# Every second step's key products as three fp32r passes in the cache stage of a two-layer decoder step

## The chip, the cores and the metric

The kernel runs on one core of a Trainium2 chip. The metric is device microseconds of one execution, first to last work of the program; the numbers of runs are medians. Instructions of five engines run side by side: TensorE (PE, its weight loads PEld), VectorE (DVE), ScalarE (ACT), GpSimd (POOL) and SyncE (SP). Each engine takes its own queue in order.

## The reference, cut to what matters

Two layers; in each, 1024 prompt tokens and 8 samples of 4 tokens. The stage that is changed is the samples' attention over a paged cache of 8192 positions:

```python
def key_nope(ckv, w_uk, kn_g):                      # ckv: [..., 128], w_uk: [128, 4*64]
    k = (ckv @ w_uk).reshape(ckv.shape[:-1] + (N_HEADS, NOPE))
    return rmsnorm(k, kn_g)                         # over the 64 of a head, fp32
...
def step(carry, pt):                                # over pages
    lat = cache_latent[layer, pt]; krp = cache_krope[layer, pt]
    kn = key_nope(lat, w_uk, kn_g)
    s = attn_scores(qn, qr, kn, krp)                # qn.kn + qr.kr, times a scale
    ... running max, exp, sums; acc += p @ lat
```

So each cached latent (128 numbers) is multiplied by `w_uk`, the mean square of its 64 numbers per head is taken, and its score with 4 heads x 4 tokens = 16 queries is scaled by the root of that. The 16 scores come out of the same product: the query is folded into `w_uk` beforehand, which gives 16 more columns.

## The kernel before, in words

A cache stage (`sample_attn`) stands in each layer between the projections and the prompt's attention. It works on 16 units (`u`), half a sample's cache each: 4096 latents, gathered by an indirect DMA on GpSimd's queue into one of 8 large slots, once as `latc` (for turning) and once as `lat` (for the value product), with the rotary keys `kr`. A unit has 8 steps (`q`, `tau = 8u + q`), a step 4 tiles of 128 latents:

- `T`: VectorE turns 512 columns of `latc` into `lT`, three steps ahead.
- `K`: per tile one fp32 product of `lT` with `WK` (256 key columns and 16 query columns, `KPC` = 272), two tiles to a pair of PSUM banks `kproj` (three such pairs). An fp32 product is two PE instructions in the trace, an fp32r product one. ScalarE squares the 256 into `sq`, `nope` copies the 16 scores into `nope`.
- `tree`: GpSimd adds the two halves of each head's squares; `red`: VectorE sums the rest into `ms`.

Around these, work of the unit before (`hp`) and of the one before that (`hpp`) is laid in at fixed steps: `krT`, `lnexp`, `newton`, `rope` (rotary scores, PE), `scale` (GpSimd), `addrope`, `colmax`, `maxT`, `bcast`, `expo`; then `expo_act`, `rowsum`, `pv` (the value product, PE), `pvend`. In layer 0 every second unit up to 13 also does a piece of the modulation weights (`ada_step`: 16 PE instructions at step 4, a copy at 5, four turns at 6). Units 13 to 15 prepare the prompt's first head (`warm`). The order is written out by hand (a manual schedule): every engine's queue is the program's order. Helpers `add`, `sub`, `mul` take the engine as last argument (`v` VectorE, `g` GpSimd) and show as L104; `act` shows as L101.

Some parts of the kernel already use three fp32r passes in place of an fp32 product: `split` copies a high part with ScalarE and subtracts it for the low part; `mm3` does high x high, high x low, low x high (L214 to L216).

Of the kernel before, what the change touches and what calls it, by code (L numbers as in the profile page):

```python
# [23 lines left out]
NT = 4  # L24
# [23 lines left out]
def _build(nc, tc, a, ctx):  # L48
# [105 lines left out]
    WKR = cp.tile([128, 2, 256], F32R, name="WKR")  # L154
    WK = [cp.tile([128, KPC], F32, name=f"WK{i}") for i in range(2)]
# [123 lines left out]
    def load_small_w(l, r, wp, pool):  # L279
# [8 lines left out]
        split(WKR[:, 0], WKR[:, 1], w[:, 768:1024])  # L288
        for i in range(2):
            v.tensor_copy(WK[i][:, 0:256], w[:, 768:1024])  # L290
# [41 lines left out]
    def mla_tile(l, r, raw, rc, m, pool, qk, cT_, nxt, vout=None):  # L332
# [18 lines left out]
        mm3(pk[:, 0:256], cT_[:, 0, sl], cT_[:, 1, sl], WKR[:, 0], WKR[:, 1])  # L351
# [129 lines left out]
    def sample_attn(l, keep, pool, warm):  # L481
# [4 lines left out]
        pbuf = [keep.tile([128, 528], F32, tag=f"p{i}", name=f"p{i}") for i in range(2)]  # L486
# [21 lines left out]
        def gather_kr(u):  # L508
            if u < NU:
                if not krs:  # L510
                    krs.append(slot("krs"))
                H[u].kr = krs[0][:, u % 4, 0:1024]
                rows(u, H[u].kr, "kr")

        def new_wk(b):
            if b < NB:
                v.tensor_copy(WK[b % 2][:, 256:KPC], S.qa[:, b].rearrange("p h t -> p (h t)"))

        def T(tau):
            if tau >= NU * NSTEP:  # L520
                return
            h, q = H[tau // NSTEP], tau % NSTEP
            h.lT = getattr(h, "lT", {})
            h.lT[q] = pool.tile([128, 512], F32, tag="lT", name="lT", bufs=4)
            v.transpose(h.lT[q], h.latc[:, 512 * q:512 * q + 512])  # L525
            if q == NSTEP - 1:
                h.latc = None

        def K(h, q, j):
            if q == 0 and j == 0:  # L530
                h.nope = keep.tile([128, 32, NH, NT], F32, tag="nope", name="nope", bufs=3)
                h.ms = keep.tile([128, 32, NH], F32, tag="ms", name="ms", bufs=2)
            if j == 0:
                h.sq = pool.tile([128, 4, 256], F32, tag="sq", name="sq", bufs=3)
            wk = WK[h.b % 2]
            kp = ps2("kproj")
            lT = h.lT[q]
            for i in range(2):
                t = 2 * j + i
                sl = slice(t * 128, (t + 1) * 128)  # L540
# [8 lines left out]
        def tree(h, q):  # L549
            sv = h.sq.rearrange("p n (h x d) -> p (n h) x d", h=NH, x=2)  # L550
            t32 = pool.tile([128, 16, 32], F32, tag="t32", name="t32", bufs=3)
            add(t32, sv[:, :, 0, :], sv[:, :, 1, :], g)
            halves.append((h, q, t32))

        def red():
            h, q, t32 = halves.pop(0)
            v.tensor_reduce(h.ms[:, 4 * q:4 * q + 4, :].rearrange("p n (h o) -> p (n h) o", o=1), t32, AX.X, ALU.add)  # L557

        def krT(h, c):
            t = pool.tile([128, 512], F32, tag="krT", name="krT", bufs=2)  # L560
            v.transpose(t, h.kr[:, 512 * c:512 * c + 512])
            h.krT = getattr(h, "krT", []) + [t]

        def rope(h, c):
            if c == 0:
                h.pr = (psr if h is H.get(NU - 1) else psm)("ropesc")
            for k in range(4):
                o = 64 * (4 * c + k)
                te.matmul(h.pr[:, o:o + 64], h.krT[c][:, 128 * k:128 * k + 128], BD[:, h.b, :], start=True, stop=True)  # L569

        def lnexp(h):
            h.t0 = keep.tile([128, 32, NH], F32, tag="ta", name="ta", bufs=2)
            act(h.t0, h.ms, AF.Ln, scale=1.0 / NOPE, bias=epsT)
            act(h.t0, h.t0, AF.Exp, scale=-0.5)

        def newton(h):
            h.rs = keep.tile([128, 32, NH], F32, tag="rs", name="rs", bufs=2)
            mul(h.rs, h.t0, h.t0)
# [24 lines left out]
        def expo(h, u):  # L603
            scv = h.sc.rearrange("p (n r) -> p n r", r=16)
            sub(scv, scv, h.pm[:, 128:144].unsqueeze(1).to_broadcast([128, 32, 16]))

        def expo_act(h, u):
            act(pbuf[u % 2][:, 0:512], h.sc, AF.Exp)

        def rowsum(h, u):  # L610
            v.tensor_reduce(RS[:, u % 2, :, u // 2, :].unsqueeze(3),
                            pbuf[u % 2][:, 0:512].rearrange("p (n h t) -> p h t n", h=NH, t=NT), AX.X, ALU.add)

        def pv(h, u, q):
            p = pbuf[u % 2]
            if q == 0:
                h.po = (psm if u == NU - 2 else psr)("po")
            for j in range(4):
                t = 4 * q + j
                te.matmul(h.po[32 * j:32 * j + 32, 0:128], p[:, 16 * t:16 * t + 32], h.lat[:, t * 128:(t + 1) * 128],  # L620
                          start=(q == 0), stop=(q == 7))

        def pvend(h, u):
            v.tensor_copy(O[:, u, :], h.po[:, 0:128])
# [5 lines left out]
        def ada_step(u, q):  # L630
# [10 lines left out]
            elif q == 5:  # L641
                A.mg = pool.tile([128, 512], F32, tag="adamg", name="adamg")
# [7 lines left out]
        gather_kr(1)  # L650
        new_wk(0)
        T(0)
        T(1)
        T(2)
        new_wk(1)
        for i in range(2):
            v.memset(pbuf[i][:, 512:528], 0.0)
        for tau in range(NSTEP * NU):
            u, q = divmod(tau, NSTEP)
            h, pu = H[u], u - 1  # L660
# [4 lines left out]
            if tau > 1:  # L665
                red()
            if hp is not None:
                if q < 2:
                    krT(hp, q)
# [8 lines left out]
            nope(h, q, 1, kp)  # L678
            if hp is not None:
                if q == 1:  # L680
                    lnexp(hp)
                elif q in (2, 3):
                    rope(hp, q - 2)
                    if q == 2:
                        scale(hp)
                elif q == 6:
                    maxT(hp, pu)
                elif q == 7:
                    bcast(hp, pu)
                    expo(hp, pu)  # L690
            if hpp is not None:
                if q == 0:
                    expo_act(hpp, u - 2)
                elif q == 3:
                    rowsum(hpp, u - 2)
                    for i in range(8):
                        pv(hpp, u - 2, i)
                elif q == 4:
# [7 lines left out]
            if u == NU - 1 and q in (4, 6):  # L706
                krT(h, q // 2 - 2)
# [5 lines left out]
        def tail():  # L713
# [3 lines left out]
            red()  # L717
# [977 lines left out]
```

## Time and profile before

| | us |
|---|---|
| median of 3 runs (range) | 1606.57 (1605.94 to 1606.84) |
| the profiled execution's own time | 1606.35 |
| its span in the trace | 1604.6 |
| cache stage of layer 0, of layer 1, first to last key product | 320.8 to 634.9, 1111.0 to 1408.1 |
| PE busy | 1547.2 (96%) |
| VectorE, ScalarE, GpSimd busy | 1122.6, 790.4, 743.8 |

The profile's spans of matmuls overlap one another, because the engine is pipelined: what one costs is read from start to start. A span of VectorE or GpSimd may hold time in which the instruction was held up.

### The profile page before, as it was taken

What the parts mean: (1) busy time and instruction counts of PE and PEld (TensorE: products, weight loads), DVE (VectorE), ACT (ScalarE), POOL (GpSimd) and SP (SyncE); (2) the same over time, 40 slices, a digit from 0 to 9 for tenths busy, and PEclk for the clock granted to TensorE, in tenths of its full rate; (3) what the DMA queues carried; (4) which work ended last, traced back from release to release, by engine and by line L of the source; (5) the groups of instructions that cost most, each with busy time, mean ns of one, the idle gap of its engine ahead of it and who ended that gap; (6) DMA issues with size and microseconds to landing.
All of it is one profiled execution on the core that took longest, in us unless ns stands there. A gap on an engine that the chain in (4) does not pass through costs nothing.

```text
span 1604.6 us, 28029 instructions
## 1 busy us (share of the span) xinstructions
PE 1547.2 (96%) x10576; PEld 1386.7 (86%) x10576; DVE 1122.6 (70%) x2131; ACT 790.4 (49%) x1935; POOL 743.8 (46%) x594
## 2 busy tenths in 40 slices
PE   4899999999999999999998999999999999989999
PEld 2799999977777888889987999998888888878999
DVE  7746755578888888684268477546899999967522
ACT  4444444365555556583145344334666665657500
POOL 3311211276666667364444021223777777746520
PEclk8999999999999999999999999999999999999999
DMA  9202223567777775213522112314666666541242
GB/s 385 56 20 70 64 77 73 171 273 281 297 285 281 287 272 192 59 47 121 202 90 70 41 40 73 78 60 153 243 260 260 261 261 251 206 125 48 68 160 82
DMA packets 79557, 254.48 MB, mean 159 GB/s; under 512 B 25472, under 2 KB 49088, under 8 KB 69184
## 3 DMA queue, kind: packets, MB, share of 16 engines
q0 software_dynamic: 13824, 151.00, 23.7%
q1 hardware_dynamic: 65600, 101.69, 20.0%
q8 instruction: 85, 1.39, 0.3%
q14 instruction: 48, 0.39, 0.1%
HBM read 231.87 MB, written 20.80 MB: 157 GB/s over the span
## 4 chain that ended last, share of the span: by engine, by line
PE 87%; DVE 6%; DMA 2%; issue 2%; ACT 1%; POOL 1%; SPq 0%; DVEq 0%; POOLq 0%; ACTq 0%
PE kproj L541 29%; PE po L620 4%; PE ropesc L569 3%; PE outa L198 2%; PE outa L200 2%; PE outa L196 2%; PE PTp L166 2%; PE rawps L216 2%; PE rawps L214 2%; PE rawps L215 2%; PE pvo L214 1%; DMA src<-qscr 1%; PE outb L200 1%; PE outb L196 1%; PE outb L198 1%
## 5 line engine op out<-in xcount | busy, mean ns | idle before, releaser
L541 PE MATMUL kproj<-WK,lT 128*128 128x272 f32 x2048 | 497.5, 397 | 3.9 <-DVE lT L525 3.9
L541 PEld LDWEIGHTS kproj<-WK,lT 128*128 128x128 f32 x2048 | 378.9, 190 | 90.0 <-issue 15.9
L101 ACT ACTIVATE sq<-kproj 128x512 f32<-128x512 f32 x512 | 305.3, 597 | 252.0 <-PE kproj L541 248.9
L104 POOL TENSOR_TENSOR t<-sq 128x512 f32<-128x512 f32 x256 | 322.3, 1274 | 138.3 <-ACT nope L547 108.3
L104 POOL TENSOR_TENSOR wt<-wraw,wt 128x1024 fp32r<-128x1024 f32 x44 | 106.9, 2431 | 312.4 <-ACT wt L116 308.3
L525 DVE STREAM_TRANSPOSE lT<-latc 128x512 f32<-128x512 f32 x256 | 177.4, 694 | 35.7 <-PE kproj L541 31.9
L557 DVE TENSOR_REDUCE ms<-t 128x16 f32<-128x512 f32 x256 | 167.0, 652 | 10.8 <-POOL t L104 10.5
L116 ACT CAST wt<-wraw 128x1024 fp32r<-128x1024 f32 x44 | 46.7, 1064 | 125.1 <-PE outb L200 81.2
L547 ACT COPY nope<-kproj 128x32 f32<-128x32 f32 x512 | 93.0, 182 | 0.6 <-DMA qscr<-qkm 0.6
L104 POOL TENSOR_TENSOR kn<-raw,ones 128x128 f32<-128x128 f32 x18 | 13.0, 723 | 163.6 <-DVE raw L104 88.2
L1365 PE MATMUL zma<-hT,wt 128*128 128x352 f32 x192 | 49.9, 366 | 26.8 <-ACT hT L1145 18.9
L569 PEld LDWEIGHTS ropesc<-BD,krT 128*128 128x128 f32 x512 | 66.8, 192 | 4.7
L886 DVE TENSOR_REDUCE pmx<-sc 128x1 f32<-128x128 f32 (+3 forms) x64 | 48.1, 751 | 26.7 <-PE pvo L166 23.5
L1365 PEld LDWEIGHTS zma<-hT,wt 128*128 128x128 f32 x192 | 36.9, 214 | 33.6 <-ACT hT L1145 21.6
L104 DVE TENSOR_TENSOR PT<-PTp,PT 128x512 fp32r<-128x512 f32 (+2 forms) x96 | 50.2, 551 | 21.8 <-ACT PT L929 20.8
L929 ACT CAST PT<-PTp 128x512 fp32r<-128x512 f32 (+2 forms) x96 | 42.8, 481 | 45.9 <-PE PTp L166 45.4
L569 PE MATMUL ropesc<-BD,krT 128*128 128x64 f32 x512 | 64.0, 268 | 0.0
L620 PE MATMUL po<-lat,p 128*32 128x128 f32 x2048 | 62.5, 274 | 0.0
L104 POOL TENSOR_TENSOR qkT<-src,qkT 96x512 fp32r<-96x512 f32 x32 | 40.9, 1279 | 33.6 <-ACT qkT L832 33.3
L620 PEld LDWEIGHTS po<-lat,p 128*32 128x32 f32 x2048 | 53.9, 110 | 2.1
L104 POOL TENSOR_TENSOR nope<-nope,rs 128x512 f32<-128x512 f32 x32 | 35.2, 1100 | 35.2 <-DVE rs L581 35.2
L101 ACT ACTIVATE P<-sc,pmx 128x128 f32<-128x128 f32 (+3 forms) x64 | 47.9, 749 | 6.9 <-DVE pmx L886 6.3
(452 smaller groups left out, 3906.2 us busy)
## 6 DMA issues: line engine op xcount, KB each, us to landing
wada<-in_w_ada SPq DMA_DIRECT2D x11, 2048.0 KB, 8.0
wraw<-in_w_in SPq DMA_DIRECT2D x32, 512.0 KB, 3.8
wraw<-in_w_out SPq DMA_DIRECT2D x14, 512.0 KB, 5.1
qscr<-qkm SPq DMA_DIRECT2D x32, 192.0 KB, 2.1
xo<-in_xT SPq DMA_DIRECT2D x8, 528.0 KB, 5.3
xscr<-xn SPq DMA_DIRECT2D x8, 528.0 KB, 3.0
xo<-xscr SPq DMA_DIRECT2D x8, 528.0 KB, 5.6
vscr<-Vm SPq DMA_DIRECT2D x16, 256.0 KB, 2.0
```

The costliest lines, as they stand in the source:

```text
L101: s.activation(out, in_, func, **k)
L104: (e or v).tensor_tensor(out, x, y, op)
L196: te.matmul(outs[n], wt[:, 0, k, :], hi[:, n * CH:(n + 1) * CH], start=(k == 0), stop=False)
L198: te.matmul(outs[n], wt[:, 0, k, :], lo[:, n * CH:(n + 1) * CH], start=False, stop=False)
L200: te.matmul(outs[n], wt[:, 1, k, :], hi[:, n * CH:(n + 1) * CH], start=False, stop=(k == 7))
L525: v.transpose(h.lT[q], h.latc[:, 512 * q:512 * q + 512])
L541: te.matmul(kp[:, i, 0:KPC], lT[:, sl], wk, start=True, stop=True)
L547: s.copy(h.nope[:, t0:t0 + 2].rearrange("p n h t -> p n (h t)"), kp[:, :, 256:KPC])
L557: v.tensor_reduce(h.ms[:, 4 * q:4 * q + 4, :].rearrange("p n (h o) -> p (n h) o", o=1), t32, AX.X, ALU.add)
L569: te.matmul(h.pr[:, o:o + 64], h.krT[c][:, 128 * k:128 * k + 128], BD[:, h.b, :], start=True, stop=True)
L620: te.matmul(h.po[32 * j:32 * j + 32, 0:128], p[:, 16 * t:16 * t + 32], h.lat[:, t * 128:(t + 1) * 128], start=(q == 0), stop=(q == 7))
L1365: te.matmul(o, zmw[j][:, i // 2, k, :], (lo if i == 1 else hi)[:, c], start=(k == 0 and i == 0), stop=(k == 7 and i == 1))
```

## The change

The diff does these things in `sample_attn`: latents are turned 1024 columns (two steps) at a time; of each such pair the first step keeps the fp32 product, the second step's half is split into `hi` (ScalarE) and `lo` (VectorE for the pairs 0 and 1 of a unit, GpSimd for 2 and 3) and goes through `mm3` against a split weight `WKR`; scores are kept query-major (`[128, 16, 32]`); `red` works on two steps at once; the first square of `newton` moves to ScalarE; `pvend`'s copy moves to ScalarE; `rope`, `pv` and `pvend` come at steps 2, 2 and 3; the gathers come at steps 3 (`lat`), 6 (`latc`) and 0 (`kr`, one unit later); `sq` has 2 buffers instead of 3, the probabilities one instead of two. Cut to its core:

```diff
-                H[u].kr = krs[0][:, u % 4, 0:1024]
+                H[u].kr = krs[0][:, u % 2, 0:1024]
...
-            h.lT[q] = pool.tile([128, 512], F32, tag="lT", name="lT", bufs=4)
-            v.transpose(h.lT[q], h.latc[:, 512 * q:512 * q + 512])
+        def T(x):
+                h, k = H[x // 4], x % 4
+                h.lT[k] = pool.tile([128, 1024], F32, tag="lT", name="lT", bufs=2)
+                v.transpose(h.lT[k], h.latc[:, 1024 * k:1024 * k + 1024])
+        def upper(x):
+                h.hi[k] = pool.tile([128, 512], F32R, tag="hi", name="hi", bufs=2)
+                s.copy(h.hi[k], h.lT[k][:, 512:1024])
+        def lower(x):
+                h.lo[k] = pool.tile([128, 512], F32R, tag="lo", name="lo", bufs=2)
+                sub(h.lo[k], h.lT[k][:, 512:1024], f(h.hi[k]), (v, v, g, g)[k])
...
             for i in range(2):
-                te.matmul(kp[:, i, 0:KPC], lT[:, sl], wk, start=True, stop=True)
+                if q % 2:
+                    mm3(kp[:, i, 0:KPC], h.hi[k][:, sl], h.lo[k][:, sl], wr[:, 0], wr[:, 1])
+                else:
+                    te.matmul(kp[:, i, 0:KPC], h.lT[k][:, sl], wk, start=True, stop=True)
...
-            s.copy(h.nope[:, t0:t0 + 2].rearrange("p n h t -> p n (h t)"), kp[:, :, 256:KPC])
+            s.copy(h.nope[:, :, t0:t0 + 2].rearrange("p r n -> p n r"), kp[:, :, 256:KPC])
...
+            pr = h.pr.rearrange("p (r n) -> p n r", r=NH * NT)
+            for k in range(8):
+                te.matmul(pr[:, 4 * k:4 * k + 4], h.krT[:, 128 * k:128 * k + 128],
+                          BD[:, h.b, :].rearrange("p (g r) -> p g r", g=4), start=True, stop=True)
...
+            act(h.rs, h.t0, AF.Square)
         def newton(h):
-            mul(h.rs, h.t0, h.t0)
...
-                te.matmul(h.po[32 * j:32 * j + 32, 0:128], p[:, 16 * t:16 * t + 32], h.lat[:, t * 128:(t + 1) * 128],
+                te.matmul(h.po[32 * j:32 * j + 32, 0:128], pw[:, :, t],
+                          h.lat[:, t * 128:(t + 1) * 128], start=(t < 4), stop=(t >= 28))
...
-            v.tensor_copy(O[:, u, :], h.po[:, 0:128])
+            s.copy(O[:, u, :], h.po[:, 0:128])
...
-            T(tau + 3)
+            if not odd:
+                T(x + 1)
+            elif x:
+                red()
             kp = K(h, q, 0)
             nope(h, q, 0, kp)
...
             kp = K(h, q, 1)
             tree(h, q)
             nope(h, q, 1, kp)
+            if odd:
+                upper(x + 1)
+                lower(x + 1)
...
                 elif q == 7:
                     bcast(hp, pu)
-                    expo(hp, pu)
+                    expo(hp)
...
-            if q == 5:
+            if q == 0 and u:
+                gather_kr(u + 1)
+            elif q == 3:
                 gather_n(u)
+            elif q == 6:
+                krT(h, 0)
                 gather_c(u + 2)
-            elif q == 7:
-                gather_kr(u + 2)
```

`x` is `tau // 2`. `krT(hp, 1)` comes at step 0, `rope`, `scale`, `rowsum` and `pv` at step 2. The weights `w_uk` are split once into `WUK`, and `WK` (fp32) and `WKR` are filled from it at the stage's start.

## Rows read from the trace of the kernel before

**Rows 1.** The page: busy time by engine, us and share of the span.
```profile
PE 1547.2 (96%) x10576; PEld 1386.7 (86%) x10576; DVE 1122.6 (70%) x2131; ACT 790.4 (49%) x1935; POOL 743.8 (46%) x594
```

**Rows 2.** Busy time by stretch; columns PE, PEld, DVE, ACT, POOL, clock, DMA.
```profile
320.80:627.00 306.20, 306.20 (x2296) 246.05 (x2296) 263.56 (x447) 184.32 (x551) 215.23 (x184) 1.00 0.70 276
1104.00:1409.00 305.00, 302.09 (x2222) 251.58 (x2220) 271.56 (x448) 187.25 (x560) 222.34 (x190) 1.00 0.61 239
```

**Rows 3.** PE's timeline over one unit of layer 1 (start, us, operation).
```profile
1141.10 0.28 PE L166 MATMUL pm<-ident,mx 128*16 128x128 f32 x1 [0.58 <-DVE mx L593]
...
1143.20 0.22 PE L601 MATMUL pm<-ident,M 16*128 16x16 f32 x1
1143.35 5.77 PE L541 MATMUL kproj<-WK,lT 128*128 128x272 f32 x24
1148.96 1.00 PE L569 MATMUL ropesc<-BD,krT 128*128 128x64 f32 x8
1149.79 2.05 PE L541 MATMUL kproj<-WK,lT 128*128 128x272 f32 x8
1151.68 1.00 PE L569 MATMUL ropesc<-BD,krT 128*128 128x64 f32 x8
1152.61 1.95 PE L620 MATMUL po<-lat,p 128*32 128x128 f32 x64
1154.50 5.77 PE L541 MATMUL kproj<-WK,lT 128*128 128x272 f32 x24
1160.10 0.27 PE L166 MATMUL pm<-ident,mx 128*16 128x128 f32 x1
```

**Rows 4.** The chain: fp32r products of 352 columns; layer 0's modulation piece.
```profile
257.12 0.32 PE bga L200 x2
...
387.02 1.85 PE adaps L235 x16
```

**Rows 5.** PE's timeline, fp32r products of 256 columns, start to start.
```profile
691.62 0.28 PE L215 MATMUL pvo<-PT,VR 128*128 128x256 f32 x1
691.74 0.28 PE L216 MATMUL pvo<-PT,VR 128*128 128x256 f32 x1
691.86 0.28 PE L214 MATMUL pvo<-PT,VR 128*128 128x256 f32 x1
```

**Rows 6.** Timeline of ScalarE and GpSimd behind one step's end, same unit.
```profile
1156.63 0.60 ACT L101 ACTIVATE sq<-kproj 128x512 f32<-128x512 f32 x1 [0.18 <-PE kproj L541]
1157.13 0.18 ACT L547 COPY nope<-kproj 128x32 f32<-128x32 f32 x1
1157.31 1.27 POOL L104 TENSOR_TENSOR t<-sq 128x512 f32<-128x512 f32 x1 [3.40 <-ACT nope L547]
```

**Rows 7.** GpSimd's timeline: trees back to back, a gather between, trees again.
```profile
411.00 1.27 POOL L104 TENSOR_TENSOR t<-sq 128x512 f32<-128x512 f32 x1 [0.56 <-ACT nope L547]
412.41 0.98 POOL L492 DMA_INDIRECT lat<-in_lat,idx  x1
414.65 2.50 POOL L104 TENSOR_TENSOR t<-sq 128x512 f32<-128x512 f32 x2
```

**Rows 8.** Groups by shape, whole span (busy us, mean ns | idle before).
```profile
L104 POOL TENSOR_TENSOR VR<-src,VR 128x512 fp32r<-128x512 f32 x16 | 20.6, 1290 | 13.4 <-ACT VR L116 13.4
L929 ACT CAST PT<-PTp 128x512 fp32r<-128x512 f32 x48 | 27.3, 588 | 25.7 <-PE PTp L166 25.4
L525 DVE STREAM_TRANSPOSE lT<-latc 128x512 f32<-128x512 f32 x256 | 177.4, 694 | 35.7 <-PE kproj L541 31.9 <-DMA latc<-in_latc,idx 2.4 <-DMA qscr<-qkm 1.5
L557 DVE TENSOR_REDUCE ms<-t 128x16 f32<-128x512 f32 x256 | 167.0, 652 | 10.8 <-POOL t L104 10.5
L593 DVE TENSOR_REDUCE mx<-nope 128x16 f32<-128x512 f32 x32 | 32.6, 1018 | 0.1
L104 DVE TENSOR_TENSOR nope<-nope,pm 128x512 f32<-128x512 f32 x32 | 21.9, 686 | 12.6 <-PE pm L601 11.9 <-issue 0.5
```

**Rows 9.** Tile `rs` (`newton`, VectorE): duration ns min/median/max.
```profile
L104 DVE TENSOR_TENSOR rs<-ta x32: 281/1956/3194, 341.9 to 1416.4; 128x128 f32<-128x128 f32 x32
L104 DVE TENSOR_TENSOR rs<-rs,ms x32: 291/293/1373, 344.1 to 1416.9; 128x128 f32<-128x128 f32 x32
```

More of the change, by code (lines that the diff above doesn't have):

```diff
@@ L287, in load_small_w @@
         split(r.wuq[:, 0], r.wuq[:, 1], wq)
-        split(WKR[:, 0], WKR[:, 1], w[:, 768:1024])
-        for i in range(2):
-            v.tensor_copy(WK[i][:, 0:256], w[:, 768:1024])
+        split(WUK[:, 0, 0:256], WUK[:, 1, 0:256], w[:, 768:1024])
         w = pool.tile([128, 8, 128], F32, tag="wraw", name="wuvraw", bufs=2).rearrange("p a b -> p (a b)")[:, 0:512]
@@ L485, in sample_attn @@
         M = keep.tile([16, NU], F32, tag="M", name="M")
-        pbuf = [keep.tile([128, 528], F32, tag=f"p{i}", name=f"p{i}") for i in range(2)]
+        pw = keep.tile([128, 32, 32], F32, tag="p", name="p")
+        v.memset(pw[:, NH * NT:], 0.0)
+        pbuf = pw[:, 0:NH * NT]
+        WK = [keep.tile([128, KPC], F32, tag=f"WK{i}", name=f"WK{i}") for i in range(2)]
+        WKR = [WUK, keep.tile([128, 2, KPC], F32R, tag="WKR", name="WKR")]
         H = {}
@@ L516, in new_wk @@
             if b < NB:
[L517 to L523, printed above, removed]
[L524 to L527 removed]
+                qa, w = S.qa[:, b].rearrange("p h t -> p (h t)"), WKR[b % 2]
@@ L559, in krT @@
         def krT(h, c):
[L560 to L569, printed above, removed]
+            h.krT = krs[0][:, 2, 0:1024]
@@ L650, in sample_attn @@
         gather_kr(1)
+        add(WK[0][:, 0:256], f(WUK[:, 0, 0:256]), f(WUK[:, 1, 0:256]))
         new_wk(0)
         T(0)
-        T(1)
-        T(2)
+        upper(0)
+        lower(0)
+        v.tensor_copy(WK[1][:, 0:256], WK[0][:, 0:256])
+        v.tensor_copy(WKR[1][:, :, 0:256], f(WUK[:, :, 0:256]))
         new_wk(1)
-        for i in range(2):
-            v.memset(pbuf[i][:, 512:528], 0.0)
         for tau in range(NSTEP * NU):
             u, q = divmod(tau, NSTEP)
+            x, odd = divmod(tau, 2)
             h, pu = H[u], u - 1
             hp, hpp = H.get(pu), H.get(u - 2)
-            T(tau + 3)
+            if not odd:
+                T(x + 1)
+            elif x:
+                red()
             kp = K(h, q, 0)
             nope(h, q, 0, kp)
-            if tau > 1:
-                red()
             if hp is not None:
-                if q < 2:
-                    krT(hp, q)
+                if q == 0:
+                    krT(hp, 1)
                 elif q == 2:
@@ L681, in sample_attn @@
                     lnexp(hp)
[L682 to L685, printed above, removed]
+                elif q == 2:
+                    rope(hp)
+                    scale(hp)
                 elif q == 6:
@@ L716, in tail @@
             red()
-            red()
+            expo_act()
+            lnexp(h)
+            rope(h)
+            h.kr = h.krT = A.mg = None
             krs.clear()
-            expo_act(hp, u - 1)
-            lnexp(h)
-            rope(h, 0)
-            rope(h, 1)
-            rowsum(hp, u - 1)
-            for i in range(8):
-                pv(hp, u - 1, i)
+            rowsum(u - 1)
+            pv(hp, u - 1)
             pvend(hp, u - 1)
@@ L737, in tail @@
             bcast(h, u)
-            expo(h, u)
+            expo(h)
             yield
-            expo_act(h, u)
+            expo_act()
             yield
-            rowsum(h, u)
+            rowsum(u)
             yield
             yield
-            for i in range(8):
-                pv(h, u, i)
+            pv(h, u)
             pvend(h, u)
```

98 lines of the change are left out of this document (54 added, 44 removed).

## The prediction

> **What bounds the kernel now.** I read the page first: PE is busy 96% of the span, VectorE 70%, GpSimd 46% [rows 1]. An average says little of a stage, so the stretches came next: in both cache stages PE is busy all but 3 us of 305, at full granted clock, while VectorE has 264 and 272 us of work there and GpSimd 215 and 222 [rows 2]. Third, PE's timeline of one unit. From one `pm` to the next it takes 1160.10 - 1141.10 = 19.00 us with 0.58 us idle once [rows 3]; so in this stage PE sets the pace, and what an engine beside it does counts only where PE comes to wait for it. The reader should see there the price of a step: three steps (24 instructions, two for each of 12 products) go from 1143.35 to 1148.96, 1.87 us a step. `rope` takes 0.83 and 0.93, the value product 1.89, `bcast` 0.15 [rows 3].
>
> **What the change gives PE.** An fp32r product of 256 columns starts 0.12 us after the one before [rows 5], one of 352 columns takes 0.16 [rows 4]; 272 columns lie a sixth of the way: 0.127 us. An odd step has 4 tiles of 3 passes, 12 x 0.127 = 1.52 us, against 1.87. Four odd steps a unit: 1.4 us, 17.6 instead of 19.0 us; over 32 units 45 us, if nothing is late.
>
> **What PE has to wait for then.** The split adds a chain that did not exist. `lower(x + 1)` is issued at the end of an odd step and its result is the third product of the next odd step. Between them PE has only one fp32 step and two products: 1.87 + 0.25 = 2.12 us. The chain, from the end of an odd step's products: the first of the three steps behind the value product ends at 1154.50 + 1.87 = 1156.37; the square of its second half starts at 1156.63, the copy at 1157.13, and GpSimd's `tree` at 1157.31 [rows 6], 0.91 us behind the end with an idle GpSimd. `upper` on ScalarE stands behind that copy, about 0.59 us [rows 8], and is done at 1.50, before the tree.
>
> Pair 2 (issued at step 3, on GpSimd): the tree is ahead of `lower` in GpSimd's queue. Back to back trees take 1.25 [rows 7], a subtraction of 128x512 into fp32r 1.29 there [rows 8]. Low part ready at 0.91 + 1.25 + 1.29 + 0.05 = 3.5, needed at 2.12: PE waits 1.4 us, then does the other ten products (1.27). From the end of step 3 to that of step 5 it takes 4.76 instead of 3.39.
>
> Pair 3 (issued at step 5, on GpSimd): behind the first subtraction stands the gather of `lat`, moved here; with one gather the next instruction of GpSimd comes some 1.12 us later (412.27 to 413.39 [rows 7]). So, from step 3's end: subtraction until 3.45, gather 4.57, tree of step 4 until 5.82, tree of step 5 until 7.07, subtraction 8.36. Low part at 8.4, step 7 ends 1.27 later, at 9.67: 4.91 us for the two steps instead of about 3.5.
>
> Pair 0 (issued at step 7, on VectorE): its input is high minus turned latents, two operands from SBUF. Such an instruction of `newton`, 0.28 us alone, takes 1.96 in the median and up to 3.19 [rows 9], in a kernel where GpSimd's trees run beside it; the reductions and turns, with one SBUF operand, keep their 0.65 and 0.69 [rows 8]. So I let the subtraction wait for the tree of step 7, which itself stands behind the tree of step 6 (until 9.6) and the gather of `latc`, moved to step 6 (10.73): tree until 11.98, subtraction of some 0.66 (a 128x512 subtraction with one PSUM operand has 0.69 [rows 8]), low part at 12.7, end of step 1 at 13.97. From step 7's end that is 4.30 instead of 3.54. Behind it in VectorE's queue stand `expo` (about 0.6) and `T` for steps 2 and 3, now 1024 columns, twice 0.63 to 0.69: done at 14.5, where step 2 wants it at 13.97. That is up to 0.58 more; I take half, because the order of the two queues can slip either way.
>
> Pair 1 (issued at step 1, on VectorE) has `rope` and `pv`, 3.65 us, both put at step 2, between it and its use. The subtraction may wait out two trees there at no cost; without that cover it would cost like pair 0. Steps 2 and 3: 1.87 + 1.76 + 1.89 + 1.52 = 7.04.
>
> [...]
>
> **The other edits.** `newton`'s first product goes to ScalarE, out of VectorE's long waits (1.96 us in the median [rows 9]); `colmax` and `rowsum` read in a row instead of at a stride: 1.02 us becomes something like the 0.65 of `red` on as many numbers [rows 8]. These free about 2.7 us of VectorE a unit against 1.4 for two subtractions: worth nothing on PE by themselves. ScalarE has 187.25/16 = 11.7 us of work a unit [rows 2] and gets 4 x 0.59 for `upper`, under 0.5 for the square and `pvend`'s copy of 128x128: 14.6, hidden behind PE's 17.6 or more. GpSimd goes from 222.34/16 = 13.9 [rows 2] to 16.5, which by its sum still fits under 17.6; it is the order that hurts, not the sum. With `sq` at two buffers the square of a step waits for the tree two steps before: step 6's square is wanted at 5.9 and that tree ends at 5.82, so it just fits. `gather_kr` at step 0 waits for VectorE's `krT` of the keys that it overwrites, and holds the tree of step 1 behind it: the cover of steps 2 and 3 takes that.
>
> Strided operands: the weights of `pv` are now read at a step of 32 numbers, and `rope` writes its 64 columns at such a step; the trace has no strided product. From below nothing (both are loads or writes beside the products). From above the ratio of the nearest row, the strided reduction against the straight one, 1018/652 = 1.56 [rows 8]: 0.56 x (1.89 + 1.76) = 2.0 us a unit. I take nothing: that row is another engine's, and `rope`'s pace of 0.1 us for 64 columns [rows 3] leaves room.
>
> **Sum.** A unit: 7.04 + 4.76 + 4.91 + 4.30 + 0.3 = 21.3 us against 19.0, +2.3, over 32 units +74. In 7 units of layer 0 the modulation's 16 instructions (1.85 us [rows 4]) stand at step 4, inside pair 2's wait of 1.4, which is then covered: -10. The start of each layer gets a longer first turn and the weight sums on VectorE ahead of the first product, about 1.5 us each (estimate: 0.65 for the second half of the turn, the rest for three small instructions): +3. Against the profiled execution's 1606.35, which stands 0.2 below the median of 1606.57: 1606.35 + 74 - 10 + 3 = 1673 us.
>
> **The rivals.**
> First, on the other side: the low parts come in time and PE stays the bound. 1606.35 - 45 + 3 = 1564. For it: GpSimd's work of 16.5 us fits under 17.6, ScalarE's and VectorE's too. Against it: the chain of one tree and one subtraction is 3.5 us with an idle GpSimd, and PE has 2.12 us to fill. It decides where all waits of a unit together fall below 1.4 us, that is, if the two GpSimd pairs wait under 0.7 each: the subtraction would have to take half of what rows 8 show, or run ahead of the tree. Chance 0.13.
>
> Second, only the GpSimd pairs wait; VectorE's subtraction finds a gap before the tree and `T` is in time: 7.04 + 4.76 + 4.91 + 3.54 = 20.25, +1.25 a unit: 1606.35 + 40 - 10 + 3 = 1639. Chance 0.25. For it: waits in `newton` are as short as 0.28 at times [rows 9].
>
> Third, as forecast, with PE's strided operands at the upper bound: 1673 + 32 x 2.0 = 1738. Chance 0.07. [...]
>
> **How the numbers follow.** My forecast has 0.52, its own range 1655 to 1700 (the unknown half of `T`'s delay and one gather's price up or down). 0.03 goes to gains and waits that cancel. The range 1590 to 1735 leaves out the first and the third rival, 0.2. Slower 0.52 + 0.25 + 0.07 = 0.84, within 0.2% (3 us, about what a measurement of this kernel can tell from no change) 0.03, faster 0.13.
>
> **What the profile after would show.** Right: products of 272 columns in threes at 0.127 us; PE idle in front of the low product (L216 form of `kproj`), about 1.4 us in steps 5 and 7, released by GpSimd's `lo`, and less in step 1, released by VectorE's; none in step 3; units of about 21 us with PE near 80% in the stage. Wrong if PE shows no idle time there, if units are under 19 us, if `pv` takes over 2.5 us, or if the clock of the stage falls below 1.00 because PE idles.

## The result, and the profile after

The changed kernel takes 1692.83 us, the median of 4 runs (1691.04 to 1696.87), against 1606.50 for the kernel before: a ratio of 1.054, 95% interval 1.052 to 1.056. The profiled execution took 1694.03 us, its span 1692.3.

The page of the changed kernel, then one stretch of layer 1's cache stage (columns as in [rows 2]):

```profile
PE 1553.5 (92%) x11088; PEld 1404.8 (83%) x11088; DVE 1141.1 (67%) x1891; ACT 866.4 (51%) x2143; POOL 831.9 (49%) x658
```

```profile
1200.00:1370.00 170.00, 148.61 (x1280) 126.58 (x1279) 138.02 (x167) 108.72 (x325) 131.56 (x111) 1.00 0.58 217
```

PE was busy all but 3 us of 305 in [rows 2]; now it is busy for 148.61 of 170 us, 87%, at the same granted clock of 1.00. No other engine is full: GpSimd has 77% and VectorE 81%. The time is in waits.

PE's timeline over one unit after, in the columns of [rows 3], shows where:

```profile
1240.27 2.07 PE L561 MATMUL kproj<-WK,lT 128*128 128x272 f32 x8
1242.18 1.89 PE L590 MATMUL ropesc<-BD,krs 128*128 128x64 f32 x16
1244.01 2.02 PE L638 MATMUL po<-lat,p 128*32 128x128 f32 x64
1245.95 0.39 PE L213 MATMUL kproj<-WUK,hi 128*128 128x272 f32 x1
...
1247.55 1.99 PE L561 MATMUL kproj<-WK,lT 128*128 128x272 f32 x8
...
1250.98 0.39 PE L215 MATMUL kproj<-WUK,lo 128*128 128x272 f32 x1 [1.18 <-POOL lo L104]
1251.21 0.29 PE L213 MATMUL kproj<-WUK,hi 128*128 128x272 f32 x1
1251.34 0.29 PE L214 MATMUL kproj<-WUK,hi 128*128 128x272 f32 x1
...
1252.35 1.99 PE L561 MATMUL kproj<-WK,lT 128*128 128x272 f32 x8
...
1255.87 0.40 PE L215 MATMUL kproj<-WUK,lo 128*128 128x272 f32 x1 [1.17 <-POOL lo L104]
...
1257.32 0.23 PE L622 MATMUL pm<-ident,M 16*128 16x16 f32 x1
1257.48 2.10 PE L561 MATMUL kproj<-WK,lT 128*128 128x272 f32 x8
...
1260.07 0.39 PE L215 MATMUL kproj<-WUK,lo 128*128 128x272 f32 x1 [0.24 <-DVE lo L104]
...
1261.92 1.38 PE L561 MATMUL kproj<-WK,lT 128*128 128x272 f32 x5
```

Each L561 row is an even step; the `pm` row of 16x16 (`bcast`) stands at the end of step 7. From mark to mark: steps 2 and 3 take 1247.55 - 1240.27 = 7.28 us, steps 4 and 5 4.80, steps 6 and 7 4.97, steps 0 and 1 4.60; together 21.65. From one `pm` to the next it was 18.94 before in most units of layer 1 and is 21.63 after. The first low product of steps 5 and 7 stands 1.18 and 1.17 us behind a low part from GpSimd, that of step 1 behind one from VectorE, that of step 3 waits for nothing.

The timeline of VectorE, ScalarE and GpSimd in the same unit shows what makes the parts late:

```profile
1248.43 1.27 POOL L104 TENSOR_TENSOR t<-sq 128x512 f32<-128x512 f32 x1 [0.83 <-ACT sq L101]
...
1249.67 1.26 POOL L104 TENSOR_TENSOR lo<-lT,hi 128x512 fp32r<-128x512 f32 x1
...
1258.18 1.27 POOL L104 TENSOR_TENSOR t<-sq 128x512 f32<-128x512 f32 x1
1258.65 1.37 DVE L104 TENSOR_TENSOR lo<-lT,hi 128x512 fp32r<-128x512 f32 x1 [2.16 <-ACT hi L538]
...
1259.94 0.67 DVE L104 TENSOR_TENSOR p<-nope,pm 128x512 f32<-128x512 f32 x1
...
1260.54 1.23 DVE L528 STREAM_TRANSPOSE lT<-latc 128x1024 f32<-128x1024 f32 x1
...
1260.65 0.21 ACT L567 COPY nope<-kproj 128x32 f32<-128x32 f32 x1 [1.29 <-DVE p L104]
```

On GpSimd the tree of step 3 and the subtraction follow one another (1248.43, 1249.67), and the low product starts 0.05 us behind their end. On VectorE the subtraction starts at 1258.65, beside a tree that began at 1258.18, and ends 0.57 us behind that tree's end at 1259.45. Behind it come `expo` (tile `p`) and the turn. The last row is a wait that the prediction had not seen: `nope` has two buffers instead of three, so ScalarE's first copy of a unit waits until `expo` has read the scores of two units before.

All low parts by tile (ns min/median/max, then first and last start), and what PE's idle time before `kproj` products waited for (us, times; PE's matmuls alone):

```profile
L104 DVE TENSOR_TENSOR lo<-lT,hi x64: 691/1386/2626, 327.9 to 1481.2; 128x512 fp32r<-128x512 f32 x64
L104 POOL TENSOR_TENSOR lo<-lT,hi x64: 1252/1267/1290, 338.9 to 1495.0; 128x512 fp32r<-128x512 f32 x64
...
  POOL lo L104: 66.7, 58
  DVE lo L104: 11.7, 32
```

**Where the 87.7 us of span went** (1692.3 - 1604.6): the 30 intervals from `pm` to `pm` +68.7 (layer 0 27.9, layer 1 40.8), the stretch from the first product to the first `pm` of each stage +10.5, PE's gap ahead of the first product +4.6 in layer 0 and +2.7 in layer 1, all else together +1.2. The gap of layer 0, VectorE's and PE's rows, then a window behind it (columns as in [rows 2]):

```profile
325.10 0.48 DVE L484 MEMSET p<- 128x512 f32 x1 [3.14 <-DMA qscr<-qkm]
325.50 0.36 DVE L104 TENSOR_TENSOR WK<-WUK 128x256 f32<-128x256 f32 x1
...
325.93 1.24 DVE L528 STREAM_TRANSPOSE lT<-latc 128x1024 f32<-128x1024 f32 x1
...
327.31 3.96 PE L561 MATMUL kproj<-WK,lT 128*128 128x272 f32 x8 [6.56 <-DVE lT L528]
```

```profile
328.00:331.00 3.00, 3.00 (x9) 2.26 (x7) 2.40 (x6) 0.70 (x2) 0.00 (x0) 0.50 0.05 19
```

VectorE stands 3.14 us until the stores `qscr<-qkm` have read memory that the stage's own tiles then take; the fp32 weights are now among these, and the first turn stands behind them. Behind the gap the granted clock is 0.50 for a while, so that the eight instructions of the first step take 3.96 us where those of later even steps take 1.99 to 2.10; in layer 1 it is 0.50 from 1154 to 1157. The kernel before has 1.00 there. This is a part of the +10.5.

### The profile page after: what moved, and what is told of

Read it like the earlier page. It is cut to its first block, busy times and chain, and to the rows that moved or that the text cites. A ratio compares the mean times of both kernels' runs of the same rounds, so it can differ in the third digit from the quotient of the medians.

```text
span 1692.3 us, 29006 instructions
## 1 busy us (share of the span) xinstructions
PE 1553.5 (92%) x11088; PEld 1404.8 (83%) x11088; DVE 1141.1 (67%) x1891; ACT 866.4 (51%) x2143; POOL 831.9 (49%) x658
## 3 DMA queue, kind: packets, MB, share of 16 engines
q8 instruction: 89, 1.46, 0.3%
## 5 line engine op out<-in xcount | busy, mean ns | idle before, releaser
L561 PE MATMUL kproj<-WK,lT 128*128 128x272 f32 x1024 | 263.8, 401 | 11.2 <-DVE lT L528 11.2
L561 PEld LDWEIGHTS kproj<-WK,lT 128*128 128x128 f32 x1024 | 186.5, 191 | 48.4 <-issue 16.6
L528 DVE STREAM_TRANSPOSE lT<-latc 128x1024 f32<-128x1024 f32 x128 | 157.7, 1232 | 0.0
L578 DVE TENSOR_REDUCE ms<-t 128x32 f32<-128x1024 f32 x128 | 152.9, 1194 | 4.9 <-POOL t L104 3.9
L104 DVE TENSOR_TENSOR lo<-lT,hi 128x512 fp32r<-128x512 f32 x64 | 106.6, 1665 | 69.2 <-ACT hi L538 69.2
L215 PE MATMUL kproj<-WUK,lo 128*128 128x272 f32 x256 | 78.0, 305 | 37.3 <-POOL lo L104 32.0
L538 ACT CAST hi<-lT 128x512 fp32r<-128x512 f32 x128 | 82.2, 642 | 25.4 <-DVE lT L528 25.4
L213 PE MATMUL kproj<-WUK,hi 128*128 128x272 f32 x256 | 85.1, 332 | 0.9
L213 PE MATMUL kproj<-WKR,hi 128*128 128x272 f32 x256 | 84.6, 330 | 1.2
L104 POOL TENSOR_TENSOR lo<-lT,hi 128x512 fp32r<-128x512 f32 x64 | 81.1, 1268 | 0.0
L214 PE MATMUL kproj<-WUK,hi 128*128 128x272 f32 x256 | 73.9, 289 | 0.0
L214 PE MATMUL kproj<-WKR,hi 128*128 128x272 f32 x256 | 73.7, 288 | 0.0
```

Of the source, the lines that this page charges most:

```text
L104: (e or v).tensor_tensor(out, x, y, op)
L213: te.matmul(out, lh, rh, start=start, stop=False)
L214: te.matmul(out, lh, rl, start=False, stop=False)
L215: te.matmul(out, ll, rh, start=False, stop=stop)
L528: v.transpose(h.lT[k], h.latc[:, 1024 * k:1024 * k + 1024])
L538: s.copy(h.hi[k], h.lT[k][:, 512:1024])
```

## The experiments

The theory: the subtraction for the low parts is the loss. GpSimd's come late because a tree runs ahead of them, VectorE's because a subtraction with two operands from SBUF waits while GpSimd runs. The rivals: the rest of the edit (layout, copies, strided operands) costs, or the split loads the engines, whoever waits for it. The times compare with the kernel before, run beside each, at 1606 to 1607 us. The letters A to D are those of each expectation.

**No subtraction.**

```diff
-                    mm3(kp[:, i, 0:KPC], h.hi[k][:, sl], h.lo[k][:, sl], wr[:, 0], wr[:, 1])
+                    mm3(kp[:, i, 0:KPC], h.hi[k][:, sl], h.hi[k][:, sl], wr[:, 0], wr[:, 1])
...
-                lower(x + 1)
```

> The changed kernel without the low part of the latents: the subtraction is gone from VectorE and GpSimd, and the third pass reads the high part again, so PE does the same passes; the result leaves out low x high. Theory A (PE waits for the subtraction behind the trees): no idle time in front of the third pass, units of 17.4 to 18.0 us instead of 21.63, about 1606 - 45 + 10 for the later starts = 1570 to 1590 us. Rival B (the changed stage is held by the load of the other engines, by ScalarE's copies or the order of the queues): units stay above 19.5 us, over 1630 us.

1590.06 us, ratio 0.989 (0.988 to 0.991), 103 us under the changed kernel and at the upper end of A's range. Units of layer 1 alternate between 17.65 to 17.75 and 20.07 to 20.10 (the last long one 19.31). The short ones are what the prediction gave for a PE that waits for nothing, 17.6. In the long ones this happens (timeline, VectorE and PE):

```profile
1237.36 2.97 DVE L104 TENSOR_TENSOR WUK<-qa,WUK 128x16 fp32r<-128x16 f32 x1 [2.68 <-ACT WUK L116]
...
1242.10 0.28 PE L165 MATMUL pm<-ident,mx 128*16 128x128 f32 x1 [2.27 <-DVE mx L614]
```

Every second unit `new_wk` splits the query columns of the next sample; its subtraction of 16 columns waits 2.68 us for ScalarE's copy and is then held for 2.97, beside the issue of a gather and two trees on GpSimd. `colmax` (`mx`) is late, and PE waits. Even so this version beats the kernel before: the passes and the rest of the edit together are a gain of 17 us, the subtraction for the latents is the loss.

**Split made but not used.** The odd steps go back to one fp32 product; the split still runs.

```diff
-                    mm3(kp[:, i, 0:KPC], h.hi[k][:, sl], h.lo[k][:, sl], wr[:, 0], wr[:, 1])
+                    te.matmul(kp[:, i, 0:KPC], h.lT[k][:, 512 + sl.start:512 + sl.stop], wk, start=True, stop=True)
```

> The changed kernel with fp32 products in the odd steps too: the split still runs on ScalarE, VectorE and GpSimd, but nothing reads it. Theory A: PE never waits for it, units of 18.9 to 19.4 us as before the change, 1612 to 1630 us with the later starts. Rival B (the work of the split itself, GpSimd's sum or the shared reads, holds the stage): units above 20.3 us, over 1655 us.

1659.87 us, ratio 1.033 (1.031 to 1.035); units of 19.67 in layer 1, a pair of 42.46 in layer 0 (before: 18.94 and 40.37). The time is that of B, the units lie between the two. No PE product waits for a low part here, and still a unit is 0.7 us longer than before the change in layer 1 and 1.0 in layer 0. How much of that is the split's load, the next run tells. VectorE's low parts take up to 4.42 us.

**No split at all**: fp32 in every step as in the run above, and the calls of `upper` and `lower` left out too.

> The changed kernel with fp32 products in the odd steps and no split at all: what is left of the change are the turns of two steps, the query-major scores, the moved gathers and copies, and the fewer buffers. Theory A (these parts cost nothing on PE, the later start of a stage apart): units of 18.9 to 19.1 us, 1606 to 1616 us. Rival B (strided operands of the value product and of the rotary scores, or the buffers, hold PE): units above 19.4 us, over 1622 us.

1622.92 us, ratio 1.011 (1.009 to 1.013). Units of layer 1 alternate 19.07 and 19.90. So the layout alone costs 0.13 us in a unit, and every second one pays 0.8 for `new_wk`: its subtraction of 16 columns is held for 1.77 us there, and PE waits 0.73 for `mx`. The numbers, with gaps of 5.90 and 5.23 us at the starts, just reach B's (19.5 in the mean of two units, over 1622), but not for B's reason: the short units leave no more than 0.13 for strided operands and buffers. Against this row the split's load in the run before costs 37 us. From trace to trace it is 39.6, and it lies unevenly: 13.2 in the first 13 intervals between `pm` in layer 0, 1.0 a unit; 4.0 in those of layer 1, 0.3 a unit; 16.8 in the last two intervals of the two stages, where the prompt's first head is prepared as well.

**The low part one step earlier**, all four:

```diff
-            if odd:
+            if not odd:
                 upper(x + 1)
                 lower(x + 1)
```

> The changed kernel with the split of a pair issued at the end of the even step before, one step earlier, so that it stands behind the even step's tree and ahead of the odd step's. Theory A: GpSimd's chain is 3.5 us from the even step's end, PE has 1.52 + 2.12 = 3.64 us to fill: waits in steps 5 and 7 under 0.3 us each, units of 17.8 to 19.0 us, 1580 to 1615 us. Rival B (sum of GpSimd's work): the waits only move, units above 20 us, over 1645 us.

1706.54 us, ratio 1.062 (1.061 to 1.064). A's gain did not come, as B had it. PE's wait for GpSimd's low parts falls from 66.7 to 9.4 us, but VectorE's subtraction at step 6 now runs into two trees and holds up `M`, for which PE waits (timeline):

```profile
1257.52 2.22 DVE L104 TENSOR_TENSOR lo<-lT,hi 128x512 fp32r<-128x512 f32 x1 [1.44 <-ACT hi L538]
...
1259.99 0.22 PE L622 MATMUL pm<-ident,M 16*128 16x16 f32 x1 [1.68 <-DVE M L619]
```

In every second unit of layer 1 PE also waits some 3.5 us for `mx`, behind a `new_wk` whose subtraction is held for 3.66 us, and from 1200 to 1370 us the granted clock is 0.96.

**Only GpSimd's two one step earlier.**

```diff
-            if odd:
+            if q in (1, 2, 4, 7):
```

> The changed kernel with only GpSimd's two splits of a unit issued one step earlier (at steps 2 and 4 in place of 3 and 5); VectorE's two stay where the change put them. Theory A (each pair waits by its own chain: tree, then subtraction): the two steps of pair 2 go from 4.80 to about 3.5 us, of pair 3 from 4.97 to 3.5 to 4.0, steps 0 and 1 stay at about 4.6: units of 19.0 to 19.8 us, 1610 to 1640 us. Rival B (GpSimd's sum; whatever is taken from one pair is waited for in another): units above 20.8 us, over 1665 us.

1693.63 us, ratio 1.054 (1.052 to 1.056): no gain. The wait for GpSimd's low parts falls to 9.6 us, as A said, but that for VectorE's goes from 11.7 to 33.5, and units of layer 1 alternate between some 20.2 and 24.4, as B had it. In the long ones, on VectorE, GpSimd and PE:

```profile
1227.13 3.79 DVE L104 TENSOR_TENSOR WUK<-qa,WUK 128x16 fp32r<-128x16 f32 x1 [1.04 <-ACT WUK L116]
1227.17 1.28 POOL L104 TENSOR_TENSOR t<-sq 128x512 f32<-128x512 f32 x1
1228.39 1.28 POOL L104 TENSOR_TENSOR lo<-lT,hi 128x512 fp32r<-128x512 f32 x1
...
1229.62 1.26 POOL L104 TENSOR_TENSOR t<-sq 128x512 f32<-128x512 f32 x1
...
1232.69 0.38 PE L165 MATMUL pm<-ident,mx 128*16 128x128 f32 x1 [3.60 <-DVE mx L614]
```

VectorE's 16 columns end at 1230.92, at the end of the third GpSimd instruction in a row. PE stands 3.60 us, and what follows on it is slow as well. Two windows of 1 us (columns as in [rows 2]), then PE's rows:

```profile
1234.00:1235.00 1.00, 1.00 (x7) 1.00 (x6) 1.00 (x2) 0.41 (x1) 0.56 (x1) 0.50 0.00 0
...
1236.00:1237.00 1.00, 1.00 (x5) 0.84 (x5) 0.01 (x1) 0.95 (x3) 0.56 (x1) 1.00 0.73 279
```

```profile
1233.84 0.43 PE L214 MATMUL kproj<-WKR,hi 128*128 128x272 f32 x1
1234.07 0.43 PE L215 MATMUL kproj<-WKR,lo 128*128 128x272 f32 x1
```

Behind the wait the granted clock is 0.50, and the passes of step 7 start 0.23 us apart instead of 0.125: 12 x 0.1 = 1.2 us more in this unit. From 1277 to 1283 and from 1321 to 1327, at and behind the waits of the next two long units, the clock is 0.50 too.

**The same, with the copy of `new_wk` on VectorE** instead of ScalarE:

```diff
-                split(w[:, 0, 256:KPC], w[:, 1, 256:KPC], qa)
+                v.tensor_copy(w[:, 0, 256:KPC], qa)
+                sub(w[:, 1, 256:KPC], qa, f(w[:, 0, 256:KPC]))
...
-            if odd:
+            if q in (1, 2, 4, 7):
```

> GpSimd's two splits one step earlier, as in the run before, and the 16 query columns of the split weight, made anew for each sample at step 4 of every second unit, with both halves on VectorE, so that VectorE does not wait there for a copy behind ScalarE's queue. Theory C (that wait is what made every second unit 4 us longer once GpSimd's low parts were in time): all units 19.1 to 20.3 us, 1615 to 1650 us. Rival B (GpSimd's and VectorE's sums with the shared reads): the long units stay above 22.5 us, over 1670 us.

1694.33 us, ratio 1.056 (1.053 to 1.058): theory C fell, and B's numbers came. There is no wait for ScalarE left, and the long units are still 24.7. Now the first copy of `new_wk` is held, one with a single operand (timeline):

```profile
1223.40 0.97 POOL L493 DMA_INDIRECT lat<-in_lat,idx  x1
...
1224.03 4.10 DVE L519 COPY WK<-qa 128x16 f32<-128x16 f32 x1
1224.39 1.28 POOL L104 TENSOR_TENSOR t<-sq 128x512 f32<-128x512 f32 x1
1225.62 1.26 POOL L104 TENSOR_TENSOR lo<-lT,hi 128x512 fp32r<-128x512 f32 x1
...
1226.84 1.24 POOL L104 TENSOR_TENSOR t<-sq 128x512 f32<-128x512 f32 x1
```

It starts beside the issue of a gather and ends at 1228.13, 0.05 behind the third of the instructions that follow. By tile it lasts 156/1586/4101 ns (min, median, max) here; in the changed kernel, at another place among the trees, 152/157/171.

**Third `nope` buffer.** (To make room, `ta` and `rs` get one buffer each.)

```diff
-                h.nope = keep.tile([128, NH * NT, 32], F32, tag="nope", name="nope", bufs=2)
+                h.nope = keep.tile([128, NH * NT, 32], F32, tag="nope", name="nope", bufs=3)
```

> The changed kernel with three buffers of scores instead of two (the root's two small tiles get one buffer each for the room). Theory A1 (in steps 0 and 1 ScalarE's first copy of a unit's scores waits until expo of the unit two before has read its buffer, and expo stands behind the subtraction on VectorE): those two steps go from 4.60 to about 4.3 us or less, 1680 to 1686 us. Rival A2 (the late turn on VectorE holds them whatever the buffers): no change, 1691 to 1695 us.

1694.78 us, ratio 1.055 (1.053 to 1.056), units unchanged at 21.63. ScalarE's wait for `expo` is gone, but the turn for step 2 starts no earlier, at 1241.64 where that unit's subtraction started at 1239.74 and `expo` at 1241.05, and PE's step 2 at 1243.02, 0.15 us behind the turn's end. So ScalarE's copy and the late turn were two waits of equal length behind the same held subtraction.

**All low parts on VectorE.**

```diff
-                sub(h.lo[k], h.lT[k][:, 512:1024], f(h.hi[k]), (v, v, g, g)[k])
+                sub(h.lo[k], h.lT[k][:, 512:1024], f(h.hi[k]), v)
```

> The changed kernel with all four subtractions of a unit on VectorE. Theory A (VectorE is held for the one tree that runs and then needs 0.7 us): pairs 2 and 3 wait 0.6 to 0.8 us in place of 1.2 to 1.4, GpSimd is 2.5 us a unit lighter: units of 20.3 to 21.0 us, 1655 to 1675 us. Rival B (VectorE is passed over by one tree after another, and its turns and reductions come late behind it): units above 21.6 us, over 1690 us.

1656.56 us, ratio 1.031 (1.029 to 1.033), as A said; units of layer 1 20.03 and 20.79. PE's waits for low parts are a little shorter than A had them: 33.8 us in 60 waits, 0.56 each. The chain of tree and subtraction on one queue, with GpSimd's share of the load, is worth 36 us, and what VectorE pays in its place (1.27 us in the median for a low part) is less; but units of 20.0 are still longer than the 18.94 with fp32 in all steps.

**A low part with one operand.** VectorE's two are made by a reduction of the same size that reads `hi` alone.

```diff
-                sub(h.lo[k], h.lT[k][:, 512:1024], f(h.hi[k]), (v, v, g, g)[k])
+                if k < 2:
+                    v.tensor_reduce(h.lo[k].unsqueeze(2), f(h.hi[k]).unsqueeze(2), AX.X, ALU.max)
+                else:
+                    sub(h.lo[k], h.lT[k][:, 512:1024], f(h.hi[k]), g)
```

> The changed kernel with VectorE's two low parts of a unit made by an instruction of the same size that reads only one operand from SBUF (a reduction over one element of the high part; the result has a wrong low part for half of the odd steps). Theory A (two SBUF operands shut VectorE out while a tree runs): each of them takes 0.6 to 0.75 us in place of 1.39 in the median and up to 2.63, steps 0 and 1 go from 4.60 to 3.6 to 4.0, units of 20.5 to 21.0 us, 1660 to 1680 us. Rival D (they wait for ScalarE's copy and their place in the queue): durations shorten, but units stay at 21.4 us or more, 1688 to 1695 us.

1668.24 us, ratio 1.039 (1.037 to 1.041). By tile, and PE's start of step 2:

```profile
L546 DVE TENSOR_REDUCE lo<-hi x64: 685/686/689, 325.8 to 1454.7; 128x512 fp32r<-128x512 f32 x64
```

```profile
1239.65 0.23 PE L625 MATMUL pm<-ident,M 16*128 16x16 f32 x1
...
1243.57 1.61 PE L564 MATMUL kproj<-WK,lT 128*128 128x272 f32 x6
```

The same size at the same place in the queue takes 0.69 us all 64 times, where the subtraction took 0.69 to 2.63 and 1.39 in the median. Steps 0 and 1 take 3.92 us instead of 4.60, a unit 20.94 instead of 21.63. A was right in all its numbers: that the subtraction is held is shown directly, and costs 0.7 us a unit. That it is the second operand which brings this on is not shown, since the reduction is another kind of instruction too, and in the run before a copy with one operand was held.

**The memset moved** from the head of the stage to behind `new_wk(1)`.

```diff
-        v.memset(pw[:, NH * NT:], 0.0)
...
         new_wk(1)
+        v.memset(pw[:, NH * NT:], 0.0)
```

> The changed kernel with the clearing of the probabilities' tile moved behind the first turn and split. Theory A (that clearing, first in VectorE's queue, waits for a store that still reads the memory it lies on, and the first turn stands behind it): PE's gap at the start of the stage goes from 6.6 us to 3 or 4 in layer 0 and from 4.8 to 3 or so in layer 1, 1686 to 1690 us. Rival B (something else of the start is waited for): no change, 1691 to 1695 us.

1695.91 us, ratio 1.056 (1.054 to 1.058); the gap of layer 0 stays at 6.51. A fell: the next write into the stage's own memory, the sum for `WK`, then waits for the same store.

**Three passes in step 3 alone.** The split is issued at step 1 only, where `rope` and `pv` stand between it and its use; fp32 elsewhere; `new_wk` on VectorE as above.

```diff
-                if q % 2:
+                if q == 3:
...
-            if odd:
+            if q == 1:
                 upper(x + 1)
                 lower(x + 1)
```

> Three passes in step 3 alone, the one whose low part has rotary scores and value product (3.7 us) as cover; fp32 in the other odd steps; the new query columns wholly on VectorE. Theory A: no wait for the low part, PE gains 0.35 us a unit over the version without any split, units of 18.6 to 18.9 us, 1603 to 1615 us with the later start of a stage. Rival B (VectorE's held subtraction makes turns late all the same): units above 19.2 us, over 1622 us.

1608.41 us, ratio 1.002 (1.001 to 1.003), as A said. Units of layer 1 take 18.67, 0.40 less than the short units without a split (19.07) where 0.35 was expected, and 0.27 less than before the change (18.94); those of layer 0 19.10 and 20.73 against 19.38 and 20.99. VectorE's low part still takes 1.84 us in the median, and PE no longer sees it. The gain of some 8 us goes back at the starts: the gaps are 7.97 and 5.25 us, 1.96 each before.

**The same, with the old start.** `WK` lies in permanent memory and is filled with the other weights as before; the clearing and the second set of weights come after the first turn.

```diff
+    WK = [cp.tile([128, KPC], F32, name=f"WK{i}") for i in range(2)]
...
+        for i in range(2):
+            v.tensor_copy(WK[i][:, 0:256], w[:, 768:1024])
...
-        add(WK[0][:, 0:256], f(WUK[:, 0, 0:256]), f(WUK[:, 1, 0:256]))
-        new_wk(0)
+        v.tensor_copy(WK[0][:, 256:KPC], S.qa[:, 0].rearrange("p h t -> p (h t)"))
         T(0)
```

> Three passes in step 3 alone, as in the run before, with the fp32 weights held for the whole program and filled early, as they were before the change, and the first turn ahead of everything that lies on memory still being read. Theory A (what that version loses is the later start of a stage alone): PE's gap at the start falls to 2 to 4 us in both layers, units stay at 18.67, 1596 to 1604 us, faster than the kernel before. Rival: the start is held by another wait, 1606 to 1610 us.

1600.34 us (6 runs, 1598.05 to 1602.74) against 1606.72 (11 runs, 1603.81 to 1609.31), ratio 0.996 (0.994 to 0.997). It beats both kernels, the one before by a little. PE's first products of the two stages:

```profile
321.03 7.43 PE L566 MATMUL kproj<-WK,lT 128*128 128x272 f32 x24 [2.50 <-DVE lT L533]
...
1112.66 5.74 PE L566 MATMUL kproj<-WK,lT 128*128 128x272 f32 x24 [2.50 <-DVE lT L533]
```

Both gaps are 2.50 us, the units stay at 18.67, as A said. The same three steps take 7.43 us in layer 0 and 5.74 in layer 1; the granted clock is 0.50 from 323 to 325 us and 1.00 from 1113 to 1116.

## Why the prediction was right, point by point

**Direction and size.** 1673 was forecast, with 1655 to 1700 as the range of that case; 1692.83 was measured. Of the 20 us between, the longer units make 32 x 0.39 = 12.5 and the starts some 8; the modulation takes 2.5 off (terms below).

**PE's gain of 1.4 us a unit**: right. Passes start 0.125 us apart (1251.21 to 1251.34) against 0.127, and without the subtraction units of 17.65 appear, forecast 17.6. The kernel never sees this gain, since what a unit loses by its waits, about 18.94 - 17.65 + 2.69 = 4.0 us, is three times as large. PE is busy for 87% of the stretch, where "near 80%" was forecast.

**Pairs 2 and 3** (GpSimd): 4.76 and 4.91 us forecast, 4.80 and 4.97 measured, each with 1.2 us of idle PE in front of the low product. The chain worked from [rows 6] to [rows 8] holds almost to the digit: the low part of pair 2 is used 3.43 us behind step 3's end, forecast 3.5, and the ten products behind it take 1.37 us instead of 1.27.

**Pair 0** (VectorE): 4.30 + 0.3 forecast, 4.60 measured, by a partly other way; that the sum agrees to the digit is luck, for the 0.3 was the half of a bound. The subtraction waits for the tree, as argued (it ends 0.57 us behind it in the unit above), and the one-operand run shows that this costs 0.7 us (a unit of 21.63 against 20.94). But behind it stood two waits of equal length, the turn and ScalarE's copy into `nope`; the second was overlooked, though the diff takes `nope` from three buffers to two.

**Pair 1** under the cover of `rope` and `pv`: right, no wait. Steps 2 and 3 took 7.28 against 7.04. The strided operands, taken at nothing with a bound of 2.0 us a unit, cost some 0.1: `pv` 1.94 instead of 1.89, `rope` 1.83 instead of 1.76. The third rival, which had the 2.0, is out: the strided write of `rope` adds 0.07 us to 1.76 here, for fp32 products of 64 columns, and the strided weights of `pv` 0.05 to 1.89.

**The mis-sized terms.** A unit: +2.3 forecast, +2.69 measured. The four stretches make +0.34 of that difference (21.65 against 21.31), 0.24 of it in steps 2 and 3. The starts: "about 1.5 us each (estimate)", +3, where the gaps alone cost 4.6 + 2.7 = 7.3. On top of them come the first two steps at the lower clock, 5.40 us (327.31 to 332.71) and 5.07 (1153.43 to 1158.50) in place of 3.39: 3.7. The prediction names a clock below 1.00 in the stage as a sign of being wrong; it came behind the two start gaps, not behind the waits that the forecast is made of. The estimate counted instructions, and the cost was in the main a wait: the fp32 weights had moved into the stage's own memory, and the stores `qscr<-qkm` still read there. That the last run gets both gaps down to 2.50 by moving the weights back and the rest behind the first turn shows it, for the two edits together. Modulation: -10 forecast; layer 0's intervals grew by 15 x 2.69 - 27.9 = 12.5 less than at layer 1's rate. In units of layer 0 without the piece PE waits for GpSimd's parts as in layer 1 (1.16 us at 474.33, 1.19 at 513.21); in the one between, with the piece at 489.57, it does not wait at step 5 and waits 0.59 at step 7. So the piece covers pair 2's wait, as forecast, and its four turns cover half of pair 3's besides.

**A step of the reasoning that is not borne out**: "it is the order that hurts, not the sum". Two other orders put GpSimd's parts nearly in time (66.7 us of wait become 9.4 and 9.6) and gained nothing, 1706.54 and 1693.63. VectorE was then held beside what GpSimd did in one go (3.79 us beside three instructions in the second), so the wait changed place, and where PE's wait came to 3.60 us the clock of 0.50 behind it took another 1.2. And the load costs where nobody waits for the parts: 1659.87 against 1622.92.

**The rivals.** The first, low parts in time, would have given 1564; neither reordering reached it. Only the run that leaves out the subtraction came near, 1590.06: of the 26 us left, six units of some 20.1 and one of 19.3 in layer 1 make 6 x 2.4 + 1.7 = 16, and the starts, where the gaps alone cost 5.4 + 2.7 us, most of the rest. The second, with VectorE's subtraction out of the tree's way, comes nearest in the one-operand run: 20.94 a unit, 1668.24, not 20.25 and 1639. Steps 0 and 1 take 3.92 there where the rival had 3.54, and steps 2 and 3 7.29 where it had 7.04; the gaps of the starts cost 4.9 + 3.0 us instead of 3.

What stays open: why the split's load costs 1.0 us a unit in layer 0, 0.3 in layer 1 and far more in the last units of a stage was not tried.

## What to carry to other kernels

A cheaper operation that needs a new operand is to be priced by the chain that makes this operand against the time until its use, engine queue by engine queue, and not by the engine that it relieves: here 0.35 us saved a step stood against a chain of 3.5 us with 2.1 us to fill. Make the change only where other work of the bound engine already lies over the chain (step 3 here); applied to a quarter of its places, with `new_wk` on VectorE and the old start, it won 0.4%, applied everywhere it lost 5.4%. Before a tile moves to a stage's own memory, look at what still reads that memory when the stage starts, and at what stands in the queue behind the first write into it.

## What the runs showed of the hardware that was not expected

**A VectorE instruction was held beside three GpSimd instructions in a row.** The subtraction of pair 0 above ended 0.57 us behind the end of one tree. But a copy of 16 columns lasted 4.10 us, and a subtraction of 16 columns 3.79, both begun during a gather's issue with three GpSimd instructions back to back behind it (from 1224.39 to 1228.08 and from 1227.17 to 1230.88). These two ended 0.05 and 0.04 us behind the third of them, where GpSimd's queue has its first gap (1.60 and 1.32 us). It was not always so. In the one-operand run the same copy began inside a tree and ended at 1211.14, 0.02 us behind that tree, though the next GpSimd instruction followed without a gap (timeline):

```profile
1210.45 0.69 DVE L519 COPY WK<-qa 128x16 f32<-128x16 f32 x1
...
1209.85 1.27 POOL L104 TENSOR_TENSOR t<-sq 128x512 f32<-128x512 f32 x1 [1.41 <-ACT sq L101]
1211.08 1.26 POOL L104 TENSOR_TENSOR lo<-lT,hi 128x512 fp32r<-128x512 f32 x1
```

What decides between the two was not tried.

**A copy with one operand was held like a subtraction with two** (156 ns at best, 4101 at worst); this one goes from SBUF to SBUF. One reduction and the turns were not: the reduction of the one-operand run took 685 to 689 ns in 64 of 64, and the turns of the run with that copy 1223 to 1245 in 128 of 128.

**PE's lower clock came behind some of its waits, and their length alone did not tell behind which.** From 1200 to 1370 us of the changed kernel PE waits 1.2 us twice a unit and idles 13%, and the granted clock stays at 1.00. In the run without the subtraction PE waits 2.26 or 2.27 us in six units of layer 1. Behind five of these waits the clock stayed at 1.00, behind the sixth, at 1355.54, it fell to 0.50. Windows behind the fifth and the sixth:

```profile
1318.00:1321.00 3.00, 3.00 (x20) 2.63 (x20) 3.00 (x5) 1.93 (x6) 2.18 (x3) 1.00 0.90 295
1357.00:1360.00 3.00, 3.00 (x9) 2.25 (x9) 3.00 (x4) 1.62 (x5) 1.68 (x2) 0.50 0.99 421
```

In the run with the copy of `new_wk` on VectorE it fell behind a wait of 1.46 us (at 431.29; 0.50 from 433 to 435), in the last run behind one of the two gaps of 2.50 us and not behind the other. At the wait of 3.60 us above it fell before PE started again at 1232.69 (1.00 from 1231 to 1232, 0.51 from 1232 to 1233), stayed at 0.50 until 1235 and was back at 1.00 by 1236; over the stretch from 1200 to 1370 us of that run 0.94 was granted.
